# Storing the last two rows of the last batch through SyncE, widened by ScalarE, behind the first nine rows

## The chip, the cores and the metric

One core of a Trainium2 chip. The metric is device time in microseconds (us) of one execution. The profile's span is about 1.8 us shorter than that time. The sets of experiments ran on different chips (numbers 13, 2 and 6 in the record), so a ratio compares only runs of the same set.

## The reference, cut to what matters

```python
# x: (8, 2048, 16, 64) float32; cos, sin: (2048, 32) float32
x1, x2 = x[..., :32], x[..., 32:]
out1 = x1 * cos - x2 * sin
out2 = x1 * sin + x2 * cos
return np.concatenate([out1, out2], axis=-1).astype(np.float32)
```

Input and output are 67.1 MB each in float32. The arithmetic is six operations for each pair of elements.

## The kernel before

Each batch is one tile of 128 partitions x 16 rows x 1024 elements, held in float16. GpSimd's DMA queue (its software ring, "the ring" below) narrows float32 to float16 on the load and widens it on the store. VectorE does four passes for each batch. Five tiles rotate. In the code P is the 128 partitions, J the 16 rows of a partition, H x D = 16 x 64 the 1024 elements of a row.

```python
def load(b):                        # float32 in HBM -> float16 in SBUF
    xt = io_pool.tile([P, J, H, D], f16)
    j0 = JA if b == 0 else 0        # JA = 2: rows 0 and 1 of batch 0 come through SyncE
    nc.gpsimd.dma_start(out=xt[:, j0:J, :, :]..., in_=x[b]...[:, j0:J, :]...)
    return xt

def store(b, xt):                   # float16 in SBUF -> float32 in HBM
    nc.gpsimd.dma_start(out=out[b].rearrange("(p j) h d -> p (j h d)", j=J), in_=xt)

# ... rotate(xt): four VectorE passes over the tile; head: a [P, 2, H, D] float32 tile, loaded by SyncE ...
tiles = [load(b) for b in range(NBUF)]          # NBUF = 5
nc.scalar.copy(out=tiles[0][:, 0:JA, :, :]..., in_=head...)
# ... sin, -sin and cos to float16 on ScalarE ...
for b in range(B):
    rotate(tiles[b])
    store(b, tiles[b])
    if b + NBUF < B:
        tiles.append(load(b + NBUF))
```

A semaphore is a counter by which engines and transfers report that something is done. A transfer is said to land when its semaphore gets the last of its updates. A transfer is cut into packets, the pieces that the trace records for the DMA engines.

Behind this code the compiler puts a closing sequence. SyncE waits for every semaphore in use, up to two in each instruction. Then a barrier joins the engines, semaphores are cleared, a second barrier follows, and the span ends.

Of the kernel before, what the change touches and what calls it, by code (L numbers as in the profile page):

```python
# [1 line left out]

# [4 lines left out]


@with_exitstack  # L10
def kernel(
    ctx: ExitStack,
    tc: tile.TileContext,
    x: bass.AP,
    cos: bass.AP,
    sin: bass.AP,
    out: bass.AP,
):
    nc = tc.nc
    f16 = mybir.dt.float16  # L20
    f32 = mybir.dt.float32

    B, S, H, D = x.shape
    Dh = D // 2
    P = nc.NUM_PARTITIONS
    J = S // P
    NBUF = 5

    const_pool = ctx.enter_context(tc.tile_pool(name="rope_const", bufs=1))
    io_pool = ctx.enter_context(tc.tile_pool(name="rope_io", bufs=NBUF))  # L30
    tmp_pool = ctx.enter_context(tc.tile_pool(name="rope_tmp", bufs=1))

    JA = 2
    head = const_pool.tile([P, JA, H, D], f32)
    x0 = x[0].rearrange("(p j) h d -> p j (h d)", j=J)
    nc.sync.dma_start(  # L36
        out=head.rearrange("p j h d -> p (j h d)"),
        in_=x0[:, 0:JA, :].rearrange("p j f -> p (j f)"),
    )
    sin_f = const_pool.tile([P, J, Dh], f32)  # L40
    cos_f = const_pool.tile([P, J, Dh], f32)
    cos_h = const_pool.tile([P, J, Dh], f16)
    sin_h = const_pool.tile([P, J, Dh], f16)
    neg_h = const_pool.tile([P, J, Dh], f16)
    nc.sync.dma_start(out=sin_f, in_=sin.rearrange("(p j) d -> p j d", j=J))  # L45
    nc.sync.dma_start(out=cos_f, in_=cos.rearrange("(p j) d -> p j d", j=J))

    def load(b):
        xt = io_pool.tile([P, J, H, D], f16)
        j0 = JA if b == 0 else 0  # L50
        nc.gpsimd.dma_start(  # L51
            out=xt[:, j0:J, :, :].rearrange("p j h d -> p (j h d)"),
            in_=x[b].rearrange("(p j) h d -> p j (h d)", j=J)[:, j0:J, :].rearrange("p j f -> p (j f)"),
        )
        return xt

    def store(b, xt):
        nc.gpsimd.dma_start(  # L58
            out=out[b].rearrange("(p j) h d -> p (j h d)", j=J), in_=xt
        )  # L60

    def rotate(xt):
        v = tmp_pool.tile([P, J, H, D], f16)
        sin_b = sin_h.unsqueeze(2).to_broadcast([P, J, H, Dh])
        neg_b = neg_h.unsqueeze(2).to_broadcast([P, J, H, Dh])
        cos_b = cos_h.unsqueeze(2).to_broadcast([P, J, 2 * H, Dh])
        nc.vector.tensor_mul(out=v[:, :, :, 0:Dh], in0=xt[:, :, :, Dh:D], in1=neg_b)  # L67
        nc.vector.tensor_mul(out=v[:, :, :, Dh:D], in0=xt[:, :, :, 0:Dh], in1=sin_b)  # L68
        xw = xt.rearrange("p j h (e d) -> p j (h e) d", d=Dh)
        nc.vector.tensor_mul(out=xw, in0=xw, in1=cos_b)  # L70
        xa = xt.rearrange("p j h d -> p (j h d)")
        nc.vector.tensor_add(out=xa, in0=xa, in1=v.rearrange("p j h d -> p (j h d)"))  # L72

    tiles = [load(b) for b in range(NBUF)]
    nc.scalar.copy(  # L75
        out=tiles[0][:, 0:JA, :, :].rearrange("p j h d -> p (j h d)"),
        in_=head.rearrange("p j h d -> p (j h d)"),
    )
    nc.scalar.copy(out=sin_h, in_=sin_f)  # L79
    nc.scalar.mul(out=neg_h, in_=sin_f, mul=-1.0)  # L80
    nc.scalar.copy(out=cos_h, in_=cos_f)  # L81
    for b in range(B):
        rotate(tiles[b])
        store(b, tiles[b])
        if b + NBUF < B:
            tiles.append(load(b + NBUF))


# [1 line left out]
_INS = ['x', 'cos', 'sin']  # L90
_OUTS = [((8, 2048, 16, 64), 'float32')]


# [23 lines left out]
```

## Time and profile before

| | before |
|---|---|
| time, median of 6 runs | 318.28 us (317.87 to 318.67) |
| span of the profiled run | 316.06 us |
| VectorE busy | 209.2 us |
| one full transfer on the 16 DMA engines, load or store | 19.3 us |
| store of batch 6 landed | 295.33 us |
| last store landed | 314.63 us |
| last landing to end of span | 1.43 us |

The page of the kernel before: busy time of each engine, then the span in 40 slices with the busy tenths of the DMA engines and the bytes they moved, then the DMA queues.

```profile
span 316.1 us, 121 instructions
## 1 busy us (share of the span) xinstructions
DVE 209.2 (66%) x32; ACT 4.9 (2%) x5; POOL 8.8 (3%) x20
...
DMA  9899999999999999999999999999999999999996
GB/s 277 182 261 208 199 236 228 199 199 265 199 199 265 398 506 423 398 336 261 199 199 224 373 398 398 506 423 265 203 328 398 398 448 481 398 398 506 423 398 265
...
q0 software_dynamic: 2304, 100.14, 98.5%
q1 hardware_dynamic: 432, 1.57, 1.4%
```

The DMA engines are busy from the first slice to the last; no other engine is. The rate seems to halve in the slices of loads only because the count is of bytes written (2 bytes an element). In the packet records each engine moves a full transfer as 8 packets, one for each of 8 partitions, 2.41 us apart, loads and stores alike. That is 65,536 B / 2.41 us = 27.2 GB/s for an engine on the float32 side. The Trainium skill, "DMA: Bandwidth & Descriptors", section Specifications, gives a fabric ceiling of 435 GB/s for 16 engines, which is the same 27.2. The 134.2 MB of float32 are fixed by the problem; at 435 GB/s they take about 308.5 us (an estimate from that page's ceiling and these bytes), so little is left to win but the two ends.

The timeline of the kernel before from 262 us on (start, duration, engine, line, operation), and what SyncE's sequencer waited for over the whole run (total us, times, longest):

```profile
254.90 8.69 DVE L72 TENSOR_TENSOR xt<-xt,v 128x16384 f16<-128x16384 f16 x1
263.88 0.53 POOL L58 DMA_DIRECT2D out_dram<-xt  x1 [50.50 <-DVE xt L72]
```

```profile
SPq L112 <- DMA out_dram<-xt: 312.5, 3, 274.0
SPq L112 <- PEq L112: 1.0, 2, 0.6
SPq L101 <- PEq L101: 0.7, 1, 0.7
```

The last store is issued at 263.88, 50 us before it lands, because two stores stand ahead of it in the ring. (The engine named as releaser is only the last one seen at the barrier.)

### The profile page before, as it was taken

To read this page: it belongs to the slowest core of one execution; us is meant where nothing else is said; L and a number is where in the kernel's file an instruction comes from. 1 tells how busy PE (TensorE), PEld (TensorE's weight loads), DVE (VectorE), ACT (ScalarE), POOL (GpSimd) and SP (SyncE) were. 2 spreads that over 40 slices of the span, in tenths; PEclk is the share of its full clock that TensorE was granted. 3 is DMA by queue.
4 is the path that set the end of the run, shared out by engine and by line. 5 is a ranking of instruction groups with operands and counts; after the bars stand their busy time and mean duration, and the time that the engine had idled before them with its cause. 6 is when DMAs were issued, how large, how long until landed. Compare 5 with 4: busy or idle time off the path is not lost.

```text
span 316.1 us, 121 instructions
## 1 busy us (share of the span) xinstructions
DVE 209.2 (66%) x32; ACT 4.9 (2%) x5; POOL 8.8 (3%) x20
## 2 busy tenths in 40 slices
DVE  0009799999999999999879999990009993000000
ACT  4100000000000000000000000000000000000000
POOL 3000000000000000010000000100000000000000
DMA  9899999999999999999999999999999999999996
GB/s 277 182 261 208 199 236 228 199 199 265 199 199 265 398 506 423 398 336 261 199 199 224 373 398 398 506 423 265 203 328 398 398 448 481 398 398 506 423 398 265
DMA packets 2736, 101.71 MB, mean 322 GB/s; under 512 B 304, under 2 KB 304, under 8 KB 560
## 3 DMA queue, kind: packets, MB, share of 16 engines
q0 software_dynamic: 2304, 100.14, 98.5%
q1 hardware_dynamic: 432, 1.57, 1.4%
HBM read 67.63 MB, written 67.11 MB: 426 GB/s over the span
## 4 chain that ended last, share of the span: by engine, by line
issue 44%; DVE 14%; another core or an unknown queue 14%; DMA 10%; POOL 1%; SPq 0%; ACT 0%; POOLq 0%
DMA cos_f<-in_cos_dram 10%; DVE xt L70 6%; DVE xt L72 6%; DVE v L67 1%; DVE v L68 1%; POOL out_dram L58 1%; POOL xt L51 0%; ACT cos_h L81 0%; POOLq L112 0%; SPq L45 0%; SPq L36 0%; POOLq L58 0%
## 5 line engine op out<-in xcount | busy, mean ns | idle before, releaser
L70 DVE TENSOR_TENSOR xt<-xt,cos_h 128x16384 f16<-128x16384 f16 x8 | 69.5, 8692 | 2.0 <-ACT cos_h L81 1.7
L67 DVE TENSOR_TENSOR v<-xt,neg_h 128x8192 f16<-128x8192 f16 x8 | 35.4, 4426 | 52.2 <-DMA xt<-in_x_dram 52.0
L72 DVE TENSOR_TENSOR xt<-xt,v 128x16384 f16<-128x16384 f16 x8 | 69.5, 8692 | 0.3
L68 DVE TENSOR_TENSOR v<-xt,sin_h 128x8192 f16<-128x8192 f16 x8 | 35.4, 4419 | 0.0
L58 POOL DMA_DIRECT2D out_dram<-xt x8 | 4.3, 535 | 136.3 <-DVE xt L72 136.3
L51 POOL DMA_DIRECT2D xt<-in_x_dram x8 | 4.4, 559 | 119.1 <-DMA out_dram<-xt 118.3
L75 ACT CAST xt<-head 128x2048 f16<-128x2048 f32 x1 | 1.9, 1897 | 3.5 <-DMA head<-in_x_dram 3.5
L75 ACT ACT_TABLE_LOAD x1 | 1.3, 1283 | 0.7 <-PEq L101 0.7
L81 ACT CAST cos_h<-cos_f 128x512 f16<-128x512 f32 x1 | 0.6, 617 | 17.7 <-DMA cos_f<-in_cos_dram 17.7
L79 ACT CAST sin_h<-sin_f 128x512 f16<-128x512 f32 x1 | 0.6, 618 | 7.2 <-DMA sin_f<-in_sin_dram 7.2
L80 ACT ACTIVATE neg_h<-sin_f 128x512 f16<-128x512 f32 x1 | 0.6, 624 | 0.0
L101 POOL MEMSET const-float32-0.0<- 128x1 f32 x1 | 0.1, 98 | 0.2 <-issue 0.2
L101 POOL MEMSET const-bfloat16-1.0<- 128x1 bf16 x1 | 0.1, 101 | 0.0
L101 POOL MEMSET const-float32-1.0<- 128x1 f32 x1 | 0.1, 98 | 0.0
L101 POOL MEMSET const-uint8-127<- 128x1 uint8 x1 | 0.1, 98 | 0.0
## 6 DMA issues: line engine op xcount, KB each, us to landing
xt<-in_x_dram POOLq DMA_DIRECT2D x7, 4096.0 KB, 41.2
xt<-in_x_dram POOLq DMA_DIRECT2D x1, 3584.0 KB, 22.3
head<-in_x_dram SPq DMA_DIRECT2D x1, 1024.0 KB, 4.8
sin_f<-in_sin_dram SPq DMA_DIRECT2D x1, 256.0 KB, 13.4
cos_f<-in_cos_dram SPq DMA_DIRECT2D x1, 256.0 KB, 31.8
out_dram<-xt POOLq DMA_DIRECT2D x8, 66.0
```

What stands on the lines that cost most here:

```text
L51: nc.gpsimd.dma_start(out=xt[:, j0:J, :, :].rearrange("p j h d -> p (j h d)"), in_=x[b].rearrange("(p j) h d -> p j (h d)", j=J)[:, j0:J, ...
L58: nc.gpsimd.dma_start(out=out[b].rearrange("(p j) h d -> p (j h d)", j=J), in_=xt)
L67: nc.vector.tensor_mul(out=v[:, :, :, 0:Dh], in0=xt[:, :, :, Dh:D], in1=neg_b)
L68: nc.vector.tensor_mul(out=v[:, :, :, Dh:D], in0=xt[:, :, :, 0:Dh], in1=sin_b)
L70: nc.vector.tensor_mul(out=xw, in0=xw, in1=cos_b)
L72: nc.vector.tensor_add(out=xa, in0=xa, in1=v.rearrange("p j h d -> p (j h d)"))
L75: nc.scalar.copy(out=tiles[0][:, 0:JA, :, :].rearrange("p j h d -> p (j h d)"), in_=head.rearrange("p j h d -> p (j h d)"),)
L79: nc.scalar.copy(out=sin_h, in_=sin_f)
L80: nc.scalar.mul(out=neg_h, in_=sin_f, mul=-1.0)
L81: nc.scalar.copy(out=cos_h, in_=cos_f)
L101: nc = _bacc.Bacc("TRN2", target_bir_lowering=False, num_devices=1)
```

## The change

The intent that can be read from it: let the end of the last store be carried by a second queue. Two of its sixteen rows are widened to float32 by ScalarE into the idle `head` tile, and SyncE stores them once the first nine rows are out.

```diff
     for b in range(B):
         rotate(tiles[b])
-        store(b, tiles[b])
+        if b < B - 1:
+            store(b, tiles[b])
         if b + NBUF < B:
             tiles.append(load(b + NBUF))
+    dst, src = part(B - 1, 0, 9)                     # rows 0 to 8
+    gate = nc.gpsimd.dma_start(out=dst, in_=src)
+    dst, src = part(B - 1, 9, J - JA)                # rows 9 to 13
+    rest = nc.gpsimd.dma_start(out=dst, in_=src)
+    # ... rest stands behind gate in the ring (order only) ...
+    dst, src = part(B - 1, J - JA, J)                # rows 14 and 15
+    nc.scalar.copy(out=head.rearrange("p j h d -> p (j h d)"), in_=src)
+    end = nc.sync.dma_start(out=dst, in_=head.rearrange("p j h d -> p (j h d)"))
+    # ... end waits for gate's completion (a semaphore) ...
```

`part(b, j0, j1)` gives rows j0 to j1 of batch b in HBM and in its tile.

More of the change, by code (lines that the diff above doesn't have):

```diff
@@ L81, with part @@
     nc.scalar.copy(out=cos_h, in_=cos_f)
+    def part(b, j0, j1):
+        return (
+            out[b].rearrange("(p j) h d -> p j (h d)", j=J)[:, j0:j1, :].rearrange("p j f -> p (j f)"),
+            tiles[b][:, j0:j1, :, :].rearrange("p j h d -> p (j h d)"),
+        )
     for b in range(B):
         rotate(tiles[b])
-        store(b, tiles[b])
+        if b < B - 1:
+            store(b, tiles[b])
         if b + NBUF < B:
             tiles.append(load(b + NBUF))
+    dst, src = part(B - 1, 0, 9)
+    gate = nc.gpsimd.dma_start(out=dst, in_=src)
+    dst, src = part(B - 1, 9, J - JA)
+    rest = nc.gpsimd.dma_start(out=dst, in_=src)
+    tc.add_manual_dep(
+        rest.ins,
+        gate.ins.name,
+        mybir.DependencyInfo(mybir.DependencyClass.NoSync, mybir.DependencyReason.DATA),
+        reason="order of the ring",
+    )
+    dst, src = part(B - 1, J - JA, J)
+    nc.scalar.copy(out=head.rearrange("p j h d -> p (j h d)"), in_=src)
+    end = nc.sync.dma_start(out=dst, in_=head.rearrange("p j h d -> p (j h d)"))
+    tc.add_manual_dep(
+        end.ins,
+        gate.ins.name,
+        mybir.DependencyInfo(mybir.DependencyClass.Sync, mybir.DependencyReason.DATA),
+        reason="the last rows go out behind this part",
+    )
 _INS = ['x', 'cos', 'sin']
```

## The prediction

> **What bounds the kernel now.** The DMA engines. The page's DMA strip is at 9 from the first slice to the last, while VectorE is busy 66% of the span and ScalarE 2%. The trace's packet records show how tight this is: each of the 16 engines moves a full transfer (7 loads, 8 stores) as 8 packets, started 2.412 us apart, and the next transfer begins about 25 ns later. A full transfer takes 19.32 us whether it narrows (64 KB read per packet) or widens (64 KB written): 27.2 GB/s per engine on the wider side. That equals the fabric ceiling divided by 16 in the Trainium skill, "DMA: Bandwidth & Descriptors", section Specifications. The fifteen are 290 of 316.1 us; the rest is the first load, head, tables and 1.7 us before the first packet.
>
> The tail: VectorE's last addition ends at 263.6 us (timeline), the last store is issued at 263.9, but two stores are ahead of it in the ring; its packets run from 294.2 to 314.3 and it lands at 314.6. Its issue has about 30 us of slack.
>
> **What the change does.**
> - One store (8 MB written) becomes a 9-row and a 5-row store in the same ring and a 2-row store from SyncE's queue. Bytes written are the same. Estimates: 9/16 of 19.3 = 10.9 us; 5 rows 6.0 us; 2 rows 2.4 us.
> - Adds a ScalarE copy of 128x2048, about 1.9 us (the same-sized cast took 1.90), at 263.6, with some 40 us of slack.
> - The order of instructions shows no other movement; both split stores wait only for semaphores long done.
> - The SyncE store waits for the 9 rows: done at about 305.1, seen 0.4 us later, then 0.4 us to issue and 0.6 to 1 us to the first packet: it starts near 306.7, when about 2 of 8 five-row packets per engine are gone. Then the queues take turns.
>
> The Trainium skill, same page, section "Queues, rings and completion order", says an engine round-robins between queue rows at packet granularity. The trace agrees: during the first load each 2 KB table packet sits between two 28 KB packets, and adds 94 ns where its bytes at full rate are 75. So a second queue adds no bandwidth. The two queues end within about 1 us of each other, SyncE's last, with no idle stretch.
>
> **On the critical path** (estimates): two more completion writes, 0.05 us; 8 packets of 8 KB at 306 to 309 ns in place of 301.5, 0.05 us; six to eight queue turns of 10 to 20 ns, 0.1 us; perhaps a slow first packet (the first head packets took 0.6 to 1.1 us), 0 to 0.5 us. Sum +0.1 to +0.7; I take +0.2.
>
> **Time.** 318.4 us, 317.6 to 319.3. Faster by over 2%: 0.01; within 2%: 0.98; slower: 0.01.
>
> **What would show it.** Right: the ring's packets up to 294 us unchanged; 9-row packets 1.36 us apart, 5-row ones 0.75, 8 KB ones about 0.31 and alternating with them; the DMA share near full until the end; ScalarE's copy ends by 266; last landing within 0.7 us of 314.6. Wrong: an idle gap behind the 9 rows; SyncE's packets starting only after the 5 rows; split stores issued late; store packets shorter when both queues run.
>
> **What would make it wrong.** Float32-to-float32 packets running faster than widening ones beside the ring, which would gain up to 2 us; a late SyncE store, which would cost up to 2 to 3 us; or a different fixed time between last landing and end (1.4 us now) when the last transfer is SyncE's.

## The result, and the profile after

| | before | after |
|---|---|---|
| time, median of 6 runs each | 318.28 us (317.87 to 318.67) | 317.45 us (317.36 to 318.03) |
| ratio of fast runs | | 0.9978, 95% interval 0.9965 to 0.9990 |
| span of the profiled run | 316.06 | 315.65 |
| store of batch 6 landed | 295.33 | 295.39 |
| last landing | 314.63 (the ring) | 314.78 (SyncE; the ring at 312.35) |
| last landing to end of span | 1.43 | 0.87 |
| tail: batch 6 landed to end of span | 20.73 | 20.25 |

A ratio here is the mean time of one kernel's fast runs over that of the other's of the same rounds, so it is not quite the ratio of the medians quoted. The change is well within 2%, as predicted. But 317.45 lies 0.15 us below the stated range: a small loss was forecast (+0.2 us) and a small gain was measured.

The tail is the useful measure for what follows. The change acts only after batch 6 has landed; what varies from run to run before that (295.3 to 296.1 us for this landing, over all profiles but that of e3_no_gate, where SyncE's packets run earlier) drops out.

The page of the changed kernel, the same lines:

```profile
span 315.6 us, 126 instructions
## 1 busy us (share of the span) xinstructions
DVE 209.2 (66%) x32; ACT 6.8 (2%) x6; POOL 9.4 (3%) x21
...
DMA  9899999999999999999999999999999999999998
GB/s 278 184 261 207 200 249 216 199 199 249 216 199 266 399 424 507 399 332 233 233 199 199 390 407 399 399 532 266 199 224 507 399 399 498 432 399 399 432 424 341
...
q0 software_dynamic: 2448, 99.09, 98.0%
q1 hardware_dynamic: 576, 2.62, 2.2%
```

1.05 MB written moved from the ring to SyncE's queue, and the DMA strip ends at 8 where it ended at 6: less of the last slice passes without transfers. The timeline of the changed kernel from 262 us on, its stores with their size and the time from issue to landing, and SyncE's waits (total us, times, longest):

```profile
254.99 8.69 DVE L72 TENSOR_TENSOR xt<-xt,v 128x16384 f16<-128x16384 f16 x1
263.77 1.90 ACT L105 CAST head<-xt 128x2048 f32<-128x2048 f16 x1 [227.61 <-DVE xt L72]
263.97 0.53 POOL L95 DMA_DIRECT2D out_dram<-xt  x1 [50.50 <-DVE xt L72]
264.49 0.53 POOL L97 DMA_DIRECT2D out_dram<-xt  x1
306.36 0.35 SPq L106 DMA_DIRECT2D out_dram<-head  x1
```

```profile
out_dram<-xt POOLq DMA_DIRECT2D x1, 4608.0 KB, 42.3
...
out_dram<-xt POOLq DMA_DIRECT2D x1, 2560.0 KB, 47.9
...
out_dram<-head SPq DMA_DIRECT2D x1, 1024.0 KB, 8.4
```

```profile
SPq L106 <- DMA out_dram<-xt: 304.2, 1, 304.2
SPq L138 <- DMA out_dram<-head: 7.7, 1, 7.7
SPq L127 <- PEq L127: 0.7, 1, 0.7
SPq L138 <- PEq L138: 0.6, 2, 0.4
```

Everything up to the last transfer went as the prediction had it: the issues, ScalarE's 1.90 us with 40 us of slack, SyncE's issue at 306.4. The difference is in the last line. In the closing barriers SyncE now waited 0.6 us in place of 1.0.

The trace holds the closing instructions themselves, which the views above do not list. Those of the kernel before (start, duration, engine, instruction), where the ring's last store landed at 314.626:

```
263.862  51.459  GpSimd  DRAIN                      -> ends 315.321
314.642   0.028  Sync    wait for the last store's semaphore (and one more)
314.701 to 314.890       four more waits of Sync for semaphores long reached, 0.06 us apart
314.945   0.007  Sync    DRAIN, reports to the barrier
315.366   0.017  GpSimd  collects the reports of the barrier
```

And those of the changed kernel, where the ring's last store landed at 312.353 and SyncE's at 314.784:

```
264.379  48.711  GpSimd  DRAIN                      -> ends 313.090
314.801   0.028  Sync    wait for SyncE's store; one more wait is behind it
314.923   0.007  Sync    DRAIN, reports to the barrier
314.956   0.017  GpSimd  collects the reports of the barrier
```

GpSimd's DRAIN ends about 0.7 us after the ring's last landing in both. In the kernel before, this is after SyncE is through its waits, and the barrier stands until then. In the changed kernel it falls under SyncE's transfer. After GpSimd has collected the reports, both take the same 0.69 us to the end of the span.

### The profile page after: what moved, and what is told of

It reads as the page before. It is cut to its first block, busy times and chain, and to the rows that moved or that the text cites. A ratio compares the mean times of both kernels' runs of the same rounds, so it can differ in the third digit from the quotient of the medians.

```text
span 315.6 us, 126 instructions
## 1 busy us (share of the span) xinstructions
DVE 209.2 (66%) x32; ACT 6.8 (2%) x6; POOL 9.4 (3%) x21
## 4 chain that ended last, share of the span: by engine, by line
issue 25%; DMA 23%; DVE 21%; another core or an unknown queue 13%; POOL 1%; ACT 1%; SPq 0%; POOLq 0%; DVEq 0%; ACTq 0%
DMA xt<-in_x_dram 12%; DMA cos_f<-in_cos_dram 11%; DVE xt L70 8%; DVE xt L72 8%; DVE v L68 3%; DVE v L67 1%; ACT head L105 1%; POOL out_dram L58 1%; POOL xt L51 0%; ACT cos_h L81 0%; SPq L45 0%; SPq L36 0%; POOLq L58 0%; DVEq L67 0%
## 5 line engine op out<-in xcount | busy, mean ns | idle before, releaser
L105 ACT CAST head<-xt 128x2048 f32<-128x2048 f16 x1 | 1.9, 1897 | 227.6 <-DVE xt L72 227.6
```

The costliest lines, as they stand in the source:

```text
L105: nc.scalar.copy(out=head.rearrange("p j h d -> p (j h d)"), in_=src)
```

## The experiments

Theory to test, called the drain theory: GpSimd's closing DRAIN waits for the ring and ends 0.7 us after the ring's last landing. A last transfer that is not the ring's hides this. Rivals: the split itself helps; bytes moved off the ring, or through SyncE's queue, are cheaper; the place of the last semaphore in SyncE's list of waits decides; any last transfer from SyncE has a shorter fixed time. All kernels gave the correct result. Edits are against the changed kernel unless said otherwise.

### The changed kernel again (e1_after_again)

No edit.

> The changed kernel, unedited, for more runs and a second profile. All theories: 0.6 to 0.9 us under the kernel before (ratio about 0.998). Drain theory: GpSimd's closing DRAIN ends 0.70 to 0.75 us after the last ring store lands (about 313.1), long before SyncE's store lands (about 314.8), and the span ends 0.87 us after that landing, against 1.43 in the kernel before. SyncE's 8 KB packets again start only when the ring is empty.

Measured: 317.68 us median of 5 (317.45 to 318.08), before 317.94 on this chip (9 runs), ratio 0.9993, interval 0.9980 to 1.0005. That is 0.26 us under the kernel before, where 0.6 to 0.9 was expected: the times alone no longer separate the two. The trace repeats itself: tail 20.24, last landing to end 0.86, DRAIN 0.735 us after the ring's landing, and SyncE's packets again started only as each engine's last ring packet ended. All 11 runs of the changed kernel average 317.63, the 15 of the kernel before in the same two sets 318.07: 0.44 us apart, close to the 0.48 by which the tails differ. The first 0.8 us was partly luck.

### All three parts in the ring (e2_all_ring)

```diff
     dst, src = part(B - 1, J - JA, J)
-    nc.scalar.copy(out=head.rearrange("p j h d -> p (j h d)"), in_=src)
-    end = nc.sync.dma_start(out=dst, in_=head.rearrange("p j h d -> p (j h d)"))
-    # end waits for gate
+    end = nc.gpsimd.dma_start(out=dst, in_=src)     # in the ring, behind rest
```

> The same split 9 + 5 + 2 rows, but all three stores in GpSimd's ring, no ScalarE copy. Drain theory: the ring is last again, DRAIN ends 0.7 us after the last landing and the span 1.43 us after it: ratio to before 1.000 to 1.0005 (318.2 to 318.4 us). Theory that the split itself helps: still about 0.998. Theory of SyncE's list of closing waits (it costs 0.06 us for each wait behind the one that ends last): the last store's semaphore now has another place in the list, so the time would move by 0.1 to 0.25 us with that place; the drain theory says that it does not matter while DRAIN ends later.

Measured: 318.27 us, ratio 1.0012 (0.9999 to 1.0024; the expected range is just inside the interval); tail 20.89, last landing to end 1.50. The gain is gone, so the split is not its source. SyncE had only three waits behind the one that ended last, in place of four, and reported 0.24 us after the landing in place of 0.32. It made no difference, because DRAIN ended at 315.70, 0.54 us after SyncE's report.

### SyncE's store without its wait for nine rows (e3_no_gate)

```diff
     end = nc.sync.dma_start(out=dst, in_=head.rearrange("p j h d -> p (j h d)"))
-    tc.add_manual_dep(end.ins, gate.ins.name, ...)
```

> The changed kernel without SyncE's wait for the nine rows: its store is issued at about 265.7 us, right behind ScalarE's copy, and the ring ends last. Drain theory: the gain is lost, ratio 1.000 (+-0.0007), span 1.43 us after the last ring landing. Theory that the SyncE path moves these bytes more cheaply, or that a shorter ring helps: still about 0.998. On turn-taking: if an engine had already committed some of the ring's packets, the first 8 KB packets come 5 or more ring packets (12 us or more) after the issue and then alternate one to one with 64 KB packets; if SyncE's queue must wait for an empty ring, they come only at about 312; if it is served at once, within 1 us and one packet.

Measured: 318.30 us, ratio 1.0012 (0.9999 to 1.0024; the value is above the range expected, the interval reaches into it), last landing to end 1.46. The same bytes go by the same route as in the changed kernel, only earlier: SyncE's store landed at 297.96, the ring's last at 314.91. The gain is gone. So neither the route nor the shorter ring pays; being last does. SyncE's waits in this kernel:

```profile
SPq L106 <- ACT head L105: 263.7, 1, 263.7
SPq L132 <- DMA out_dram<-xt: 48.6, 3, 32.1
SPq L132 <- PEq L132: 1.2, 2, 0.8
SPq L121 <- PEq L121: 0.7, 1, 0.7
```

SyncE waits for ScalarE in place of the nine rows, and the closing barriers cost it 1.2 us where they cost 0.6. The trace also speaks against the place in SyncE's list as the cause by itself. The ring's last store stands in the last closing wait here, as SyncE's store does in the changed kernel, and SyncE reported 0.12 us after the landing. The end still waited for DRAIN: it ended at 315.64, 0.74 us after the landing, and GpSimd collected 0.04 us later.

On turn-taking: SyncE issued by 266.08; its first packet ran at 272.75 on the first engine, after two further ring packets of 64 KB had started on each engine. From then on the two queues took turns, about one to one: SyncE's 8 data packets for each engine ran until 290.3, while 6 to 7 ring packets started on each. (The records of its completion writes end at 297.6.) This is none of the three outcomes as laid out beforehand. It is nearest to the first, but with two further ring packets and 6.7 us in place of five and 12 us.

### One ring store of 14 rows, SyncE gated on batch 6 (e4_gate_on_batch6)

```diff
-    dst, src = part(B - 1, 0, 9);        gate = nc.gpsimd.dma_start(out=dst, in_=src)
-    dst, src = part(B - 1, 9, J - JA);   rest = nc.gpsimd.dma_start(out=dst, in_=src)
+    dst, src = part(B - 1, 0, J - JA);   rest = nc.gpsimd.dma_start(out=dst, in_=src)
     # ... ScalarE's copy and SyncE's store as they were ...
-    # end waits for gate
+    # end waits for the store of batch 6
```

> The last batch as one ring store of 14 rows (8 packets of 57 KB per engine, 2.11 us each, 294.2 to 311.1) and SyncE's 2 rows waiting for the store of batch 6 (lands about 294.7), so issued at about 295.1, arriving in the first of the 8 packets. If an engine commits 7 or more packets ahead, SyncE's packets still start at 311 when the ring is empty, SyncE ends last and the time is that of the changed kernel (ratio 0.998). If it commits 5 or 6, one or two 8 KB packets slip in before the ring's end and the rest follow it: SyncE still last, ratio 0.998. If it commits 2 or fewer, they alternate and the ring's last packet ends within 1 us of SyncE's or after it: by the drain theory the gain shrinks or goes, ratio 0.999 to 1.000.

Measured: 317.63 us, ratio 0.9989 (0.9976 to 1.0003), tail 20.22. SyncE's packets came 7.1 us after its issue, after three further ring packets, then took turns with the rest. That count was not one of the cases laid out (it fell between "2 or fewer" and "5 or 6"). SyncE still landed last, 0.9 us after the ring (314.99 and 314.08); DRAIN ended at 314.78, before SyncE's report at 315.13. The gain is there without the nine-row gate, and with one store fewer.

### The kernel before again (e5_before_again)

No edit to the kernel before.

> The kernel before, unedited, as a control and for a second profile. Ratio 1.000 within the spread of the runs. Tail, from the landing of batch 6's store to the span's end: 20.7 to 20.8 us (20.73 in the first profile, 20.25 in both profiles of the changed kernel); last landing to end 1.40 to 1.50 us, GpSimd's closing DRAIN ending 0.69 to 0.78 us after the last landing.

Measured: ratio 0.9996 (0.9983 to 1.0010), 318.08 us median of 6. The second profile gives tail 20.73, last landing to end 1.42, DRAIN 0.695 us after the landing: the same as the first to within 0.01 us.

### Four rows through SyncE (e6_four_rows)

```diff
-    dst, src = part(B - 1, 9, J - JA)
+    dst, src = part(B - 1, 9, J - 4)
-    dst, src = part(B - 1, J - JA, J)
-    nc.scalar.copy(out=head.rearrange("p j h d -> p (j h d)"), in_=src)
+    v = tmp_pool.tile([P, 4, H, D], f32)             # VectorE's scratch, free by then
+    dst, src = part(B - 1, J - 4, J)
+    nc.scalar.copy(out=v.rearrange("p j h d -> p (j h d)"), in_=src)
     # SyncE stores from v in place of head
```

> Split 9 + 3 + 4 rows, SyncE storing four rows in place of two. Drain theory: SyncE is still last, nothing more to hide: the tail stays 20.25 to 20.35 us, last landing to end 0.87 us, ratio to before 0.998 to 0.999 as the changed kernel. Theory that each byte taken from the ring to SyncE's queue saves time: twice the gain, tail 19.8 us, ratio about 0.997.

Measured: 317.75 us, ratio 0.9979 (0.9967 to 0.9991), tail 20.24. Twice the bytes off the ring give the same tail to within 0.02 us. That ends the theory of cheaper bytes.

### One row through SyncE (e7_one_row)

```diff
-    dst, src = part(B - 1, 9, J - JA)
+    dst, src = part(B - 1, 9, J - 1)
-    dst, src = part(B - 1, J - JA, J)
+    dst, src = part(B - 1, J - 1, J)                 # through head[:, 0]
```

> Split 9 + 6 + 1 rows. Drain theory: SyncE's 8 packets of 4 KB follow the empty ring and land about 1.2 us after it, still later than the ring's landing + 0.57 us at which DRAIN would begin to matter: whole gain kept, tail 20.2 to 20.3 us. Theory of bytes: half the gain, tail 20.5.

Measured: ratio 0.9986 (0.9972 to 1.0000), tail 20.23. Half the bytes, the whole gain. DRAIN ended at 315.17, SyncE reported at 315.65. (The median of 317.97 is not low: in the profiled run batch 6 had landed 0.74 us later than in that of the changed kernel, before the change has any effect.)

### A quarter of a row through SyncE (e8_quarter_row)

```diff
-    dst, src = part(B - 1, 9, J - JA)                # rows 9 to 13
+    (in words) rest: elements 9 * 1024 to 15.75 * 1024 of each partition
-    dst, src = part(B - 1, J - JA, J)
+    (in words) end: the last 256 elements of each partition
```

> Split 9 + 6.75 + 0.25 rows: SyncE's 8 packets of 1 KB land only 0.3 to 0.5 us after the ring. Drain theory: GpSimd's DRAIN now ends after SyncE has come through its waits, so it bounds the end again, but the ring lands 0.3 to 0.4 us sooner than in the kernel before: part of the gain is kept, tail 20.35 to 20.5 us, last landing of all to end 1.0 to 1.2 us. Theory that any SyncE store at the end suffices (the kind of the last transfer sets the fixed time): tail 20.25, 0.87 us from last landing to end.

Measured: 318.27 us, ratio 0.9998 (0.9984 to 1.0011), tail 20.61, a little above the range expected; last landing to end 1.21. SyncE was last here too, but only 0.26 us behind the ring (315.13 and 314.87; 0.3 to 0.5 was expected). It reported at 315.27, DRAIN ended at 315.60, and GpSimd collected at 315.65. So a last transfer from SyncE does not have a shorter fixed time as such: it must outlast the DRAIN. SyncE's waits show it:

```profile
SPq L109 <- DMA out_dram<-xt: 304.5, 1, 304.5
SPq L141 <- DMA out_dram<-head: 7.8, 1, 7.8
SPq L141 <- PEq L141: 1.0, 2, 0.5
SPq L130 <- PEq L130: 0.7, 1, 0.7
```

The closing barriers cost 1.0 us again, as in the kernel before, although the last transfer is `head`'s as in the changed kernel.

### The ring in 2-row stores, SyncE gated on batch 6 (e9_short_packets)

Against the kernel of e4_gate_on_batch6:

```diff
-    dst, src = part(B - 1, 0, J - JA)
-    rest = nc.gpsimd.dma_start(out=dst, in_=src)
+    for j in range(0, J - JA, 2):                    # seven stores, in order in the ring
+        dst, src = part(B - 1, j, j + 2)
+        parts.append(nc.gpsimd.dma_start(out=dst, in_=src))
```

> The last batch as seven ring stores of 2 rows (56 packets of 8 KB per engine, 0.31 us each, in place of 8 of 57 KB), SyncE's 2 rows gated on batch 6 as in the run where they came 7.1 us after their issue, behind three ring packets. If SyncE's packets wait behind about 160 KB or 6 to 7 us of committed ring work, they come again at about 302 to 303 us, alternate with 8 KB packets, and are done by about 309: the ring is then last, and by the drain theory the gain is gone: last landing to end 1.4 to 1.5 us, tail 20.75 to 21.0 us (six more completion writes, about 0.04 us each at most), ratio 1.000 to 1.001. If they wait behind a fixed number of three to five packets, they come within 2 us of the issue (about 298) and the ring is last as well. If they wait for an empty ring, they come at about 311.5, SyncE is last and the tail is 20.3 to 20.5 us.

Measured: 318.94 us, ratio 1.0029 (1.0012 to 1.0046), tail 21.34, last landing to end 1.68. SyncE's first packet came at 301.9, 5.8 us after the issue, behind 18 or 19 ring packets of each engine that had started meanwhile; it landed at 307.96, the ring at 315.32. So the wait is not a number of packets. Counted by the packets that started meanwhile, it was about 128, 168 and 150 KB for each engine (2 x 64, 3 x 56 and on average 18.7 x 8, in e3, e4 and this run), and in time 6.7, 7.1 and 5.8 us. Whether time or bytes set it is open. The ring was last and the gain was lost, as expected. The loss was larger than expected: six more ring stores put the landing 0.30 us later relative to batch 6 than in e4 (19.66 and 19.36), and DRAIN ended 0.94 us after the landing.

### The runs side by side

From the traces; times are us from the start of the span.

| kernel | ring lands | SyncE's store lands | DRAIN ends | SyncE reports | GpSimd collects | tail |
|---|---|---|---|---|---|---|
| before | 314.63 | | 315.32 | 314.95 | 315.37 | 20.73 |
| before again | 314.81 | | 315.51 | 315.13 | 315.55 | 20.73 |
| all in the ring | 314.93 | | 315.70 | 315.16 | 315.75 | 20.89 |
| quarter row | 314.87 | 315.13 | 315.60 | 315.27 | 315.65 | 20.61 |
| changed | 312.35 | 314.78 | 313.09 | 314.92 | 314.96 | 20.25 |
| changed again | 312.38 | 314.81 | 313.11 | 314.95 | 314.99 | 20.24 |
| gate on batch 6 | 314.08 | 314.99 | 314.78 | 315.13 | 315.16 | 20.22 |
| four rows | 310.24 | 315.08 | 310.97 | 315.22 | 315.25 | 20.24 |
| one row | 314.43 | 315.51 | 315.17 | 315.65 | 315.68 | 20.23 |

In each row GpSimd collects 0.03 to 0.05 us after the later of "DRAIN ends" and "SyncE reports". In the first four rows this is DRAIN, in the last five SyncE. (Left out: the kernel without the gate and the one with 2-row stores, where SyncE's packets ran among earlier ones or the ring was cut in seven; in both the ring and DRAIN came last, and GpSimd collected 0.04 to 0.05 us after DRAIN.)

No version beat the changed kernel by more than the spread. The one with a single 14-row store does as well with less.

## Why the prediction was wrong

**What bounds the kernel: right.** The DMA engines were busy throughout, and the issues, the ScalarE copy and the split stores had the slack that the prediction gave them.

**That a second queue adds no bandwidth: right.** From batch 6's landing to the last landing took 19.30 us before and 19.39 after. The prediction had +0.2, from extra completion writes, small packets and a slow first packet; the packets showed 0.09. The slow first packet was 0.34 us against 0.31 for the next ones.

**"Then the queues take turns": wrong, and without consequence.** In the changed kernel SyncE's packets started on every engine only when that engine had finished the ring's last packet, from 4.8 us after the issue on. The prediction had listed this as a sign of being wrong. It also had the two queues end within about 1 us of each other; they landed 2.43 us apart. The experiments show a queue that joins a busy one behind some 6 to 7 us of ring work, and then taking turns. In the changed kernel the ring ran dry first. No idle gap came of it, so nothing was lost. Nor does the gain hang on it: in e4, where the queues did take turns at the end and landed 0.9 us apart, the tail was the same (20.22).

**The step that failed** is the term that was left out of the sum: "a different fixed time between last landing and end (1.4 us now) when the last transfer is SyncE's". It was named as a risk and entered as zero. It measured 1.43 before and 0.87 after, a gain of 0.57, against 0.09 lost in the later landing: 0.48 in all, in place of the 0.2 loss. The 0.57 can be taken apart from the two traces: GpSimd collected 0.740 us after the last landing before, and 0.172 after. Had only DRAIN been out of the way, SyncE's report at 0.319 plus 0.03 would have set it, a gain of 0.39; the remaining 0.18 is SyncE's list, in which the last store's semaphore stands further back now. The first part is shown by the experiments; the second is arithmetic on the traces and was not isolated by a run.

**The evidence was there.** The wait of SyncE in the closing barriers (1.0 us) stood in the profile before, and the DRAIN that ends 0.695 us after the landing in its trace. The prediction read the 1.43 us as one block and did not ask which engine it waited for.

**How far it was off.** The forecast was 318.4 and the median 317.45. By the tail the effect is 0.48 us; the rest of the first difference is run-to-run variation that the repeat did not show again. Taken from the 318.28 of the kernel before, 0.48 us gives 317.80, inside the stated range of 317.6 to 319.3, and so are the repeat's 317.68 and the mean of all 11 runs, 317.63. That the first median fell below the range was thus partly luck. The sign of the effect, a gain in place of a loss, was forecast wrong in any case. What causes that variation, 0.8 us in the landing of batch 6 over these profiles, was not studied.

## What to carry to other kernels

When a kernel is bound by DMA to its last microsecond, look at what stands between the last landing and the end, engine by engine, before calling it fixed. Here the queue whose closing work is longest (GpSimd's ring, 0.7 us of DRAIN) should finish first, and a transfer of another queue (SyncE's here; ScalarE's was not tried), just long enough to cover that, should be last: one row of sixteen was enough and a quarter row was not. An effect of half a microsecond in 318 is seen in landmarks of the trace that repeat to 0.02 us, long before it is seen in times that vary by 1 us.

## What the Trainium skill lacked or had wrong

- "DMA: Bandwidth & Descriptors", section Issuing engines are not separate DMA queues, says that issuing from several engines saves only the sequencer's time to initiate. For bandwidth this agrees (19.30 and 19.39 us). But the choice of queue for the last transfer changed the time from last landing to end from 1.43 to 0.87 us, which the page does not mention.
- No page gives the time by which GpSimd's closing DRAIN outlasts a busy ring: 0.695 us after the ring's last landing where the last batch was one ring store (three profiles, 0.695 to 0.696), 0.735 to 0.737 with two, 0.777 with three, 0.940 with seven, so about 0.041 us for each further store.
- The same page, section Queues, rings and completion order, has an engine round-robin between queues at packet granularity. Once both were flowing the trace of e3_no_gate about agrees (8 packets to 6 or 7 on each engine). But a queue that joined a busy ring got its first packet 5.8 to 7.1 us after the end of its issue, behind 2 packets of 64 KB, 3 of 56 KB or 18 to 19 of 8 KB on each engine; the section does not give this delay.
- No page tells of SyncE's closing list of waits: they cost about 0.06 us each even for semaphores long reached, so that those behind the last landing add up (0.32 us from landing to report with four behind it, 0.14 with one).
